# Hybrid encoder on one core: rotary tables into a slab, gates' exchange between the rotary products, P4's last sum one unit sooner, memory values later

## The chip, the cores and the metric

The kernel runs on one core of one Trainium2 chip. Its engines are named here as the profile names them: PE (TensorE, matrix products; PEld is its weight load), DVE (VectorE), ACT (ScalarE), POOL (GpSimd) and SP (SyncE, which only issues transfers here). The metric is the device time in microseconds (us) of one execution, lower is better. A time of a kernel is the median of several executions.

## The reference

The kernel computes two layers of an encoder over 512 positions of width 2048. Cut to what matters here:

```python
for l in range(DEPTH):                                        # DEPTH = 2
    h = rmsnorm(x, pre_norm_g[l])
    z = h @ w_in[l]
    q_lat, kv_lat, k_pe, gb, gc, xin, q_mem, gate = split_cols(z)
    q = (rmsnorm(q_lat, q_norm_g[l]) @ w_uq[l])               # 8 heads, 128 + 64 rotary columns each
    q = concatenate([q[..., :128], apply_rope(q[..., 128:], cos, sin)])
    kv = rmsnorm(kv_lat, kv_norm_g[l]) @ w_ukv[l]             # keys and values, 8 heads
    a_out = mla_attention(q, k, v)                            # softmax over 512 positions
    c_out = short_gated_conv(gb, gc, xin, conv_w[l])
    m_out = memory_attention(q_mem, mem_n, w_mk[l], w_mv[l])  # 4 heads into 256 memory rows
    y = concatenate([a_out, c_out, m_out]) * silu(gate)
    x = x + rmsnorm(y @ w_o[l], post_norm_g[l])
```

Everything is in float32.

## The kernel before, in words

**Products in three parts.** A float32 operand is split into a rounded high part and the rest, a low part; a product is three matmuls, high x high, high x low and low x high (lines 272, 273 and 274, helper `mm3`). The high part is a cast on ACT, the low part a subtraction on DVE. For weights these are lines 189 (tile `wh`) and 190 (tile `wl`); other operands are split by `split_to` (lines 277 and 278).

**Groups, products and units.** The input projection is worked in groups of columns, two tiles of tokens at a time, with seven products of block sums, P1 to P7, in place of eight (as Strassen's method does). Each product has four units, c = 0 to 3, one for each chunk of 512 rows of the weights. A unit gives 12 matmuls of 512 columns (two token tiles, two halves of the chunk, three parts). Its weights come by `load` on SP's queue into a raw buffer (`wr`, 8 of them, line 146), or are added to a buffer by an accumulating transfer on POOL's queue (`more`). Where neither fits, two buffers are added on DVE: `sums` (line 178) ahead of the unit's split, `then` (line 199) behind it. There are three `wh` and three `wl` tiles, 8 banks for sums of products, and 19 large tiles called slabs.

**The last group, g4.** It makes the gates `ga0` and `ga1`. It has `spared` set (as has, in layer 1 alone, the second group): in P4 its last unit has its second block (B21) loaded on SP and added by line 178, where other units use an accumulating transfer. The steps of this group are numbered; a table `beside` puts other work behind steps 12 to 27. Steps 20 to 23 are P7, 24 to 27 are P4. That other work is: the latents' rows turned through an exchange (`latents_rows_out`, 32x3x128 transfers into the slabs `D1` and `D2`), their split in four parts into `H1`, `H2` (high) and `D1`, `D2` (low) by `latents_split(0..3)`, the memory keys' fetch (`mem_fetch("Km")`), the exchange of the conv-side gates (`gate_rows(3, "gm")`, 16 transfers on SP into a slab `y`), the shared rotary key's transposes (`k_rope_turn`, `krps`), and the fetch of the rotary tables (`tables_fetch`, tile `tab`, into a raw buffer).

**The mixer behind it.** `mixer` puts the first of two rotary products (`p0`, banks `qr`, weights `w_qr`), the last latents' split, the memory values' fetch (`Vm`), the second rotary product, an activation that loads ACT's table for the exponential, the rotation on DVE (`rotate0`: `first` line 1145, `second` lines 1149 and 1150, `both` lines 1154 and 1155, `away` a split and a way through DRAM to the tile `QR`), then the first query products (`qps`, tile `Q`) and the heads: four memory heads, four token tiles each, then eight latent heads. One head tile is: scores on PE (`sc`), their negated maximum on DVE (line 1260, `nm`), the exponential on ACT (line 1263), its sum's reciprocal on DVE (line 1265, `rec`), the normalisation on ACT (line 1266), transposes on PE (line 1276, `ptp`), a split of these (`PT`), and the product with the values (`o`). `y` is the gate rows times `o` (line 1291).

**What sets the order.** PE, SP and POOL run their instructions in the order in which the program puts them. On DVE and ACT a scheduler orders the instructions ahead of time; each of the two engines then runs its list in order and waits at an instruction whose input is not there. `tc.keep_in_program_order` pins an instruction into the program's order. A DMA issue whose buffer is still in use holds up everything behind it on its queue.

Of the kernel before, what the change touches and what calls it, by code (L numbers as in the profile page):

```python
# [5 lines left out]
F32 = mybir.dt.float32  # L6
# [3 lines left out]
ALU = mybir.AluOpType  # L10
# [75 lines left out]
class Program:  # L86
# [23 lines left out]
    def add(self, fn, units=(), room=0.0, ahead=None):  # L110

        self.steps.append((list(units), fn, room, self.ahead if ahead is None else ahead))
# [115 lines left out]
def encoder(tc, x, xt, mem, memt, positions, columns, conv_w, w_in, q_norm_g, w_uq, w_qr, kv_norm_g, w_ukv,  # L228
# [47 lines left out]
    def split_to(hi, lo, src):  # L276
        nc.scalar.copy(hi, src)
        nc.vector.tensor_tensor(lo, src, hi.bitcast(F32), op=ALU.subtract)
# [213 lines left out]
    def group(left, key, w, block, slot, passes, final, hold=None, by_two=False, direct=None, spared=False, once=False):  # L492
# [25 lines left out]
        def unit(q, c):  # L518
            k = lambda n: (key, n, c)

            def of(name, loads=(), more=None, sums=(), then=(), **kw):
                at = {"B11": (0, 0), "B12": (0, 1), "B21": (1, 0), "B22": (1, 1)}
                return Unit(k(name), {k(to): [block(*at[n], c)] for to, n in loads}, more and block(*at[more], c),
                            [(k(a), k(b)) for a, b in sums], [(k(a), k(b)) for a, b in then], **kw)
            if q == "P1":
                to = "P1" if apart and not keep else "T"
                return of(to, [(to, "B11")])
            if q == "P2":
                return of("P2", [("P2", "B21")])
            if q == "P4" and c == 3 and spared:  # L530
                return of("T", [("B21", "B21")], sums=[("T", "B21")])
            if q == "P4":
                return of("T", more="B21", alloc=hold, behind=(key, "B22", 3) if passes is SECOND and c > 1 else None)
            if late:
                return {"P5": lambda: of("T", [("B12", "B12")], sums=[("T", "B12")], place=place),
                        "P6": lambda: of("T", [("B22", "B22")], sums=[("T", "B22")]),
                        "P3": lambda: of("B22", then=[("B12", "B22")]),
                        "P7": lambda: of("B12")}[q]()
            if q == "P5" and (passes is STEADY or passes is FIRST):
                return of("T", [("T", "B11")] * (passes is FIRST) + [("B12", "B12")], sums=[("T", "B12")])  # L540
            if once and q in ("P6", "P3"):
                return of("T", [("B22", "B22")], sums=[("T", "B22")]) if q == "P6" else of("B22")
            return {"P5": lambda: of("T", [("T", "B11")] if apart and not keep else [], more="B12"), "P6": lambda: of("T", more="B22"),
                    "P3": lambda: of("B22", [("B22", "B22")]), "P7": lambda: of("B22", more="B12")}[q]()
# [363 lines left out]
    def mem_fetch(n, k):  # L908
        def f():
            t = slab(n, F32R)  # L910
            nc.gpsimd.dma_start(t, G[n + "d"])
            G[n] = t.rearrange("p (s i c) -> p s i c", s=2, i=k)
        return f
# [160 lines left out]
            exchange(C["D"][k].rearrange("p (c n) -> p c n", n=S)[:, :3], C["lat"][k][:, :, :12], queue, (p,))  # L1074
        return f

    def latents_split(n, C):
        def f():
            if n == 0:
                C["H"] = slab("H1", F32R), slab("H2", F32R)  # L1080
            (d1, d2), (h1, h2) = C["D"], C["H"]
            hi, lo = ((h1[:, :768], d1[:, :768]), (h1[:, 768:1536], d1[:, 768:1536]), (h1[:, 1536:], d2[:, :512]),
                      (h2[:, :1024], d2[:, 512:1536]))[n]
            split_to(hi, lo.bitcast(F32R), lo)
            if n == 2:
                k = lambda t, c: t[:, c * S:(c + 1) * S]
                l1, l2 = (d.bitcast(F32R) for d in (d1, d2))
                G["cq"] = [k(h1, c) for c in range(4)], [k(l1, c) for c in range(3)] + [k(l2, 0)]
                G["ckv"] = [k(h2, c) for c in range(2)], [k(l2, c) for c in (1, 2)]
        return f  # L1090
# [28 lines left out]
    def halves(name, dt=F32):  # L1119
        return raw_p.tile([P, 1024], dt, tag="raw", name=nm(name)).rearrange("p (s c) -> p s c", s=2)  # L1120

    def tables_fetch():
        G["tab"] = halves("tab")
        nc.gpsimd.dma_start(G["tab"].rearrange("p s c -> p (s c)"), G["tabd"])

    def q_rope_steps(l, g):
# [213 lines left out]
    def mixer(l, C, pair2, tail):  # L1340

        (p0, rotate0, fetch0), (p1, rotate1, fetch1) = (q_rope_steps(l, g) for g in range(2))
        put(p0[:1])
        add(latents_split(3, C))
        add(mem_fetch("Vm", 2))
        put(p0[1:])
        add(lambda: nc.scalar.activation(small(1, "ex"), C["ga0"][:, NT - 1][:, 0, :1], AF.Exp, scale=0.0))
        put(rotate0[:2])
        sts = [{} for _ in range(4)]
        qkv = qkv_steps(l, 0, sts[0])  # L1350
        qkv[0] += (0.0, 1)
        qkv[2] += (0.0, 0)
        put(qkv[:1])
        its = [it for i in range(4) for it in mem_head(i)]
        m = len(its)
        between = {k: [s] for k, s in zip((2, 5, 8, 10, 12), qkv[1:])}
        between.setdefault(6, []).append((gate_rows(0, "ga0", C), []))
        for k, s in zip((1, 3), rotate0[2:]):
            between.setdefault(k, []).append(s)
        between.setdefault(7, []).append((fetch0, []))  # L1360
        between.setdefault(12, []).append((gate_rows(1, "ga1", C), []))
        between[m - 2] = [(lambda: pr.prep_next(), [])]
        for pair in range(4):
            for i in range(2):
                its += mla_head(2 * pair + i, sts[pair])
            nxt = tail if pair == 3 else spread(8, qkv_steps(l, pair + 1, sts[pair + 1]))
            if pair == 0:
                nxt = dict(zip((-1, 1, 3, 4, 6, 7), nxt_steps(nxt)))
            if pair == 2:
                nxt.update(pair2)  # L1370
            for k, v in nxt.items():
                between.setdefault(m + 8 * pair + k, []).extend(v)
        between.setdefault(m + 2, []).append((conv_rows(C), []))
        late = [(4, (tables_fetch, [])), (5, p1[0]), (6, p1[1])] + list(zip((6, 7, 8, 9), rotate1)) + [(11, (fetch1, []))]
        if l + 1 < depth:
            late += zip((12, 14, 16, 17, 18, 19, 20, 21), mem_turned_steps(l + 1))
        for k, s in late:
            between.setdefault(m + k, []).append(s)
        pipeline(its, between, m)
# [169 lines left out]
    for l in range(depth):  # L1549
# [117 lines left out]
        if l == 0:  # L1667
# [22 lines left out]
            12: out_(0, 0, q=sy), 13: out_(0, 1, q=sy), 14: out_(0, 2, q=sy), 15: out_(0, 3, q=sy),  # L1690
            16: out_(1, 0, q=sy), 17: out_(1, 1, q=sy), 18: [qm_split(0, C)] + out_(1, 2, q=gp),
            19: [qm_split(1, C)] + out_(1, 3, q=gp), 20: [lambda C=C: k_rope(C)],
            21: [latents_split(0, C)], 22: [latents_split(1, C)], 24: [latents_split(2, C), mem_fetch("Km", 4)],
            25: [gate_rows(3, "gm", C)], 26: [k_rope_turn(C), tables_fetch],
        }
        for n in range(12, 28):
            put(g4[n:n + 1])
# [88 lines left out]
```

## Time and profile before

| | us |
|---|---|
| median of 3 executions | 1459.48 |
| lowest and highest of them | 1458.66, 1460.37 |
| profiled execution, its own time | 1457.07 |
| span of the profiled execution | 1455.2 |
| granted TensorE clock, mean | 0.999 |
| mean transfer rate | 205 GB/s |

The profiled execution is a single one. Its span runs from the first to the last recorded instruction; its own time has 1.9 us around that. A timeline row gives start, duration, engine, line, operation, output tile and input tiles, and the form of these; in brackets stands the idle time of the engine ahead of it and what ended that. Layer 0's P4 lies at 411 to 425 us and its memory heads begin at 433; in layer 1 the same places lie at 1134 and 1156.

### The profile page before, as it was taken

The numbers are of one execution on the slowest core, as the hardware profiler recorded it, in microseconds if no ns is written. First come the engines' busy times: TensorE is split into PE (matmuls) and PEld (weight loads), VectorE is DVE, ScalarE is ACT, GpSimd is POOL, SyncE is SP. The second block draws the span as 40 slices with busy tenths as digits, with TensorE's granted clock in tenths as the row PEclk, the third lists the DMA queues.
The fourth block names the chain that finished last, engine by engine and source line by source line (L and its number), as shares of the span: only waits on it lengthen the run. The fifth ranks groups of instructions, "written<-read, shape, count | busy, mean of one in ns | idle before, by whom it ended". The sixth has DMA issues, their size and how long they took to land.

```text
span 1455.2 us, 19537 instructions
## 1 busy us (share of the span) xinstructions
PE 1434.8 (99%) x6960; PEld 1222.0 (84%) x6960; DVE 1129.2 (78%) x1546; ACT 872.5 (60%) x1358; POOL 283.6 (19%) x321
## 2 busy tenths in 40 slices
PE   9999999999999999999999999999999999999997
PEld 8888888898877888888898888888988788888886
DVE  5899687967877778868879666977588776788687
ACT  7856345446558688654777434544465586776543
POOL 0032403032301100311210333030333001003111
PEclk9999999999999999999999999999999999999999
DMA  9999979697896482795987999696969876129973
GB/s 366 415 265 221 223 191 206 157 203 216 187 263 166 133 260 87 135 242 147 339 285 230 233 229 222 198 192 173 208 197 191 252 174 155 35 84 159 280 154 130
DMA packets 166210, 298.44 MB, mean 205 GB/s; under 512 B 13696, under 2 KB 57760, under 8 KB 162272
## 3 DMA queue, kind: packets, MB, share of 16 engines
q0 software_dynamic: 54736, 122.51, 41.5%
q1 hardware_dynamic: 111376, 174.67, 38.1%
q8 instruction: 55, 0.90, 0.2%
q14 instruction: 43, 0.35, 0.1%
HBM read 261.85 MB, written 21.63 MB: 195 GB/s over the span
## 4 chain that ended last, share of the span: by engine, by line
PE 91%; DMA 3%; DVE 3%; ACT 2%; issue 1%; SPq 1%; POOL 0%; POOLq 0%; DVEq 0%; ACTq 0%
PE P L273 22%; PE P L274 22%; PE P L272 22%; PE ptp L1276 2%; PE o L273 1%; PE o L272 1%; PE o L274 1%; PE sc L272 1%; PE sc L273 1%; PE sc L274 1%; PE qps L272 1%; PE qps L274 1%; PE sc L1258 1%; PE sc L1257 1%; PE qps L273 1%; DVE wl L190 1%
## 5 line engine op out<-in xcount | busy, mean ns | idle before, releaser
L189 ACT CAST wh<-wr 128x1024 fp32r<-128x1024 f32 (+2 forms) x436 | 444.9, 1023 | 419.5 <-PE P L274 309.7
L190 DVE TENSOR_TENSOR wl<-wr,wh 128x1024 fp32r<-128x1024 f32 (+2 forms) x436 | 514.6, 1184 | 215.8 <-ACT wh L189 213.1
L273 PE MATMUL P<-wl,S 128*128 128x512 f32 (+1 forms) x896 | 344.1, 384 | 0.2
L272 PE MATMUL P<-wh,S 128*128 128x512 f32 (+1 forms) x896 | 344.0, 384 | 0.0
L274 PE MATMUL P<-wh,S 128*128 128x512 f32 (+1 forms) x896 | 343.3, 383 | 0.0
L273 PE MATMUL P<-wl,A 128*128 128x512 f32 (+1 forms) x656 | 252.1, 384 | 2.3 <-DVE wl L190 2.3
L272 PE MATMUL P<-wh,A 128*128 128x512 f32 (+1 forms) x656 | 253.0, 386 | 0.6 <-ACT ga L589 0.6
L274 PE MATMUL P<-wh,A 128*128 128x512 f32 (+1 forms) x656 | 251.6, 384 | 0.0
L146 POOL DMA_DIRECT2D wr<-in_w_in_dram x121 | 145.2, 1200 | 411.4 <-DVE wl L190 193.8
L273 PEld LDWEIGHTS P<-wl,S 128*128 128x128 f32 x896 | 168.2, 188 | 31.1 <-DVE wl L190 1.3
L274 PEld LDWEIGHTS P<-wh,S 128*128 128x128 f32 x896 | 168.2, 188 | 30.2
L272 PEld LDWEIGHTS P<-wh,S 128*128 128x128 f32 x896 | 168.2, 188 | 30.1
L273 PEld LDWEIGHTS P<-wl,A 128*128 128x128 f32 x656 | 123.2, 188 | 25.0 <-DVE wl L190 3.5
L272 PEld LDWEIGHTS P<-wh,A 128*128 128x128 f32 x656 | 123.1, 188 | 23.2 <-ACT ga L589 1.4
L274 PEld LDWEIGHTS P<-wh,A 128*128 128x128 f32 x656 | 123.2, 188 | 22.1
L146 POOL DMA_DIRECT2D wr<-in_w_o_dram x40 | 48.5, 1259 | 298.0 <-DVE wl L190 294.3
L1263 ACT ACTIVATE P<-sc,nm 128x512 f32<-128x512 f32 (+1 forms) x96 | 59.4, 620 | 26.9 <-DVE nm L1260 26.6
L1260 DVE TENSOR_REDUCE nm<-sc 128x1 f32<-128x512 f32 (+1 forms) x96 | 56.9, 593 | 12.7 <-PE sc L1258 9.2
L1266 ACT ACTIVATE P<-P,rec 128x512 f32<-128x512 f32 (+1 forms) x96 | 61.6, 657 | 6.8 <-DVE rec L1265 6.8
L178 DVE TENSOR_TENSOR wr<-wr,wr 128x1024 f32<-128x1024 f32 (+1 forms) x47 | 55.6, 1183 | 7.2 <-DMA wr<-in_w_in_dram 6.8
L1276 PE MATMUL ptp<-identr,P 128*128 128x128 f32 x320 | 46.3, 273 | 6.6 <-ACT P L1266 6.6
L1276 PEld LDWEIGHTS ptp<-identr,P 128*128 128x128 f32 x320 | 37.9, 140 | 13.6 <-ACT P L1266 7.8
(322 smaller groups left out, 2096.9 us busy)
## 6 DMA issues: line engine op xcount, KB each, us to landing
wr<-in_w_in_dram SPq DMA_DIRECT2D x131, 512.0 KB, 4.9
wr<-in_w_in_dram POOLq DMA_DIRECT2D x97, 512.0 KB, 7.4
wr<-in_w_o_dram SPq DMA_DIRECT2D x48, 512.0 KB, 6.3
wr<-in_w_o_dram POOLq DMA_DIRECT2D x40, 512.0 KB, 7.2
wr<-in_w_in_dram SPq DMA_DIRECT2D x32, 416.0 KB, 3.7
wr<-in_w_in_dram POOLq DMA_DIRECT2D x24, 416.0 KB, 5.9
wr<-in_w_mk_dram SPq DMA_DIRECT2D x15, 512.0 KB, 8.1
wr<-in_w_mv_dram SPq DMA_DIRECT2D x15, 512.0 KB, 10.1
```

The lines of the kernel that those rows point to most:

```text
L146: engine.dma_start(dst, src, **kw)
L178: nc.vector.tensor_tensor(tiles[a], tiles[a], tiles[b], op=ALU.add)
L189: pin(nc.scalar.copy(hi[:, h], src[:, h]))
L190: pin(nc.vector.tensor_tensor(lo[:, h], src[:, h], hi[:, h].bitcast(F32), op=ALU.subtract))
L272: nc.tensor.matmul(ps, ah, bh, start=first, stop=False, **kw)
L273: nc.tensor.matmul(ps, ah, bl, start=False, stop=False, **kw)
L274: nc.tensor.matmul(ps, al, bh, start=False, stop=last, **kw)
L1257: nc.tensor.matmul(ps, q, G["KA"], start=False, stop=False)
L1260: nc.vector.tensor_reduce(nmax, ps, axis=AX.X, op=ALU.max, negate=True)
L1263: nc.scalar.activation(pt, ps, AF.Exp, bias=nmax, accum_out=tot)
L1266: nc.scalar.activation(pt, pt, AF.Copy, scale=rec)
L1276: nc.tensor.transpose(ps[:, k * P:(k + 1) * P], pt[:, k * P:(k + 1) * P], G["ident"])
```

## The change

P4's unit c = 2 of the spared groups loads the last unit's second block as well, and adds it behind its own split; unit c = 3 only splits. The rotary tables' first fetch goes into a slab and is put behind step 21 (P7) rather than 26 (P4). The memory keys' fetch goes from step 24 to 23. The exchange of `gm` goes from step 25 into the mixer, between the two rotary products. The last latents' split is pinned into program order, on both engines. A new small POOL operation reads a column of the third tile of `ga0` ahead of the memory values' fetch, so that the fetch is issued only after that tile is written.

```diff
@@ -528,7 +528,10 @@
             if q == "P2":
                 return of("P2", [("P2", "B21")])
             if q == "P4" and c == 3 and spared:
-                return of("T", [("B21", "B21")], sums=[("T", "B21")])
+                return of("T")
+            if q == "P4" and c == 2 and spared:
+                t, b = ((key, n, 3) for n in ("T", "B21"))
+                return Unit(k("T"), {b: [block(1, 0, 3)]}, block(1, 0, 2), then=[(t, b)])
             if q == "P4":
                 return of("T", more="B21", alloc=hold, behind=(key, "B22", 3) if passes is SECOND and c > 1 else None)
             if late:
@@ -1074,14 +1077,15 @@
             exchange(C["D"][k].rearrange("p (c n) -> p c n", n=S)[:, :3], C["lat"][k][:, :, :12], queue, (p,))
         return f
 
-    def latents_split(n, C):
+    def latents_split(n, C, pin=lambda ins: ins):
         def f():
             if n == 0:
                 C["H"] = slab("H1", F32R), slab("H2", F32R)
             (d1, d2), (h1, h2) = C["D"], C["H"]
             hi, lo = ((h1[:, :768], d1[:, :768]), (h1[:, 768:1536], d1[:, 768:1536]), (h1[:, 1536:], d2[:, :512]),
                       (h2[:, :1024], d2[:, 512:1536]))[n]
-            split_to(hi, lo.bitcast(F32R), lo)
+            pin(nc.scalar.copy(hi, lo))
+            pin(nc.vector.tensor_tensor(lo.bitcast(F32R), lo, hi.bitcast(F32), op=ALU.subtract))
             if n == 2:
                 k = lambda t, c: t[:, c * S:(c + 1) * S]
                 l1, l2 = (d.bitcast(F32R) for d in (d1, d2))
@@ -1119,8 +1123,8 @@
     def halves(name, dt=F32):
         return raw_p.tile([P, 1024], dt, tag="raw", name=nm(name)).rearrange("p (s c) -> p s c", s=2)
 
-    def tables_fetch():
-        G["tab"] = halves("tab")
+    def tables_fetch(first=False):
+        G["tab"] = slab("tab")[:, :1024].rearrange("p (s c) -> p s c", s=2) if first else halves("tab")
         nc.gpsimd.dma_start(G["tab"].rearrange("p s c -> p (s c)"), G["tabd"])
 
     def q_rope_steps(l, g):
@@ -1341,8 +1345,10 @@
 
         (p0, rotate0, fetch0), (p1, rotate1, fetch1) = (q_rope_steps(l, g) for g in range(2))
         put(p0[:1])
-        add(latents_split(3, C))
+        add(latents_split(3, C, tc.keep_in_program_order))
+        add(lambda: nc.gpsimd.tensor_scalar(small(1, "ms"), C["ga0"][:, 2][:, 0, :1], 1.0, None, op0=ALU.mult))
         add(mem_fetch("Vm", 2))
+        add(gate_rows(3, "gm", C))
         put(p0[1:])
         add(lambda: nc.scalar.activation(small(1, "ex"), C["ga0"][:, NT - 1][:, 0, :1], AF.Exp, scale=0.0))
         put(rotate0[:2])
@@ -1690,8 +1696,8 @@
             12: out_(0, 0, q=sy), 13: out_(0, 1, q=sy), 14: out_(0, 2, q=sy), 15: out_(0, 3, q=sy),
             16: out_(1, 0, q=sy), 17: out_(1, 1, q=sy), 18: [qm_split(0, C)] + out_(1, 2, q=gp),
             19: [qm_split(1, C)] + out_(1, 3, q=gp), 20: [lambda C=C: k_rope(C)],
-            21: [latents_split(0, C)], 22: [latents_split(1, C)], 24: [latents_split(2, C), mem_fetch("Km", 4)],
-            25: [gate_rows(3, "gm", C)], 26: [k_rope_turn(C), tables_fetch],
+            21: [latents_split(0, C), lambda: tables_fetch(True)], 22: [latents_split(1, C)],
+            23: [mem_fetch("Km", 4)], 24: [latents_split(2, C)], 26: [k_rope_turn(C)],
         }
         for n in range(12, 28):
             put(g4[n:n + 1])
```

In layer 1's second group the add keeps its place in DVE's order and only has another line (199 for 178). On PE the order is the same before and after. Three places where it differs follow, all in layer 0; layer 1 has the same. An order's row gives line, operation, output and input tiles, their shape, and how many alike follow each other.

DVE, at the end of P4. `wl160` to `wl163` are the low parts of P4's units c = 0 to 3, `wr91` is the last unit's buffer and `wr104` the block that is added to it, `D1` and `D2` are parts of the latents' split. Before:

```order
L190 TENSOR_TENSOR wl160_3582<-wr88_2871,wh160_3581 128x1024
L278 TENSOR_TENSOR D1_136_3355<-D1_136_3355,H1_144_3575 128x768
L278 TENSOR_TENSOR D2_137_3356<-D2_137_3356,H1_144_3575 128x512
L190 TENSOR_TENSOR wl161_3603<-wr89_2889,wh161_3602 128x1024
L590 SCALAR_TENSOR_TENSOR ga1_117_3039<-ga1_117_3039,ga0_116_3038 128x16x32 x2
L178 TENSOR_TENSOR wr91_2942<-wr91_2942,wr104_3496 128x1024
L939 STREAM_TRANSPOSE ga1_117_3039<-ga1_117_3039 128x16x32 x2
L190 TENSOR_TENSOR wl162_3629<-wr90_2907,wh162_3628 128x1024
L190 TENSOR_TENSOR wl163_3652<-wr91_2942,wh163_3651 128x1024
```

And in the changed kernel:

```order
L190 TENSOR_TENSOR wl160_3584<-wr88_2871,wh160_3583 128x1024
L1088 TENSOR_TENSOR D1_136_3355<-D1_136_3355,H1_144_3575 128x768
L199 TENSOR_TENSOR wr91_2942<-wr91_2942,wr104_3471 128x1024
L190 TENSOR_TENSOR wl161_3605<-wr89_2889,wh161_3604 128x1024
L593 SCALAR_TENSOR_TENSOR ga1_117_3039<-ga1_117_3039,ga0_116_3038 128x16x32 x2
L190 TENSOR_TENSOR wl162_3633<-wr90_2907,wh162_3632 128x1024
L942 STREAM_TRANSPOSE ga1_117_3039<-ga1_117_3039 128x16x32 x2
L1088 TENSOR_TENSOR D2_137_3356<-D2_137_3356,H1_144_3575 128x512
L190 TENSOR_TENSOR wl163_3654<-wr91_2942,wh163_3653 128x1024
```

The add into `wr91` has moved from between `wl161` and `wl162` to ahead of `wl161` (line 199 for 178); the `D2` part of 512 columns has moved from ahead of `wl161` to ahead of `wl163`, and the two transposes of `ga1` behind `wl162`.

DVE, where the memory heads begin. `rm` and `qr` are the rotation's tiles, `Q` the low part of the first queries, `nm` and `rec` the heads' maxima and reciprocals, `wl166` and `wl167` low parts of weights for the heads' projections. Before:

```order
L190 TENSOR_TENSOR wl166_3743<-wr107_3579,wh166_3742 128x1024
L190 TENSOR_TENSOR wl167_4170<-wr108_3599,wh167_4169 128x1024
L1260 TENSOR_REDUCE nm_159_3804<-sc_158_3800 128x1
L1145 TENSOR_TENSOR rm_155_3778<-qr_151_3746,tab_150_3715 128x1024
L278 TENSOR_TENSOR Q_156_3784<-qps_157_3785,Q_156_3784 128x512
L1149 TENSOR_TENSOR qr_151_3746<-qr_153_3763,tab_150_3715 128x512
L1150 TENSOR_TENSOR qr_153_3763<-qr_153_3763,tab_150_3715 128x512
L1265 RECIPROCAL rec_162_3809<-tot_161_3807 128x1
L1260 TENSOR_REDUCE nm_164_3816<-sc_163_3812 128x1
L1154 TENSOR_TENSOR rm_155_3778<-rm_155_3778,qr_153_3763 128x512
L1155 TENSOR_TENSOR rm_155_3778<-rm_155_3778,qr_151_3746 128x512
L1265 RECIPROCAL rec_167_3821<-tot_166_3819 128x1
```

And in the changed kernel:

```order
L190 TENSOR_TENSOR wl166_3726<-wr107_3581,wh166_3725 128x1024
L1088 TENSOR_TENSOR D2_137_3356<-D2_137_3356,H2_145_3576 128x1024
L1149 TENSOR_TENSOR rm_156_3780<-qr_150_3729,tab_146_3579 128x1024
L1153 TENSOR_TENSOR qr_150_3729<-qr_154_3765,tab_146_3579 128x512
L1154 TENSOR_TENSOR qr_154_3765<-qr_154_3765,tab_146_3579 128x512
L1159 TENSOR_TENSOR rm_156_3780<-rm_156_3780,qr_150_3729 128x512
L1158 TENSOR_TENSOR rm_156_3780<-rm_156_3780,qr_154_3765 128x512
L190 TENSOR_TENSOR wl167_4172<-wr108_3601,wh167_4171 128x1024
L278 TENSOR_TENSOR Q_157_3786<-qps_158_3787,Q_157_3786 128x512
L1264 TENSOR_REDUCE nm_160_3806<-sc_159_3802 128x1
L1264 TENSOR_REDUCE nm_165_3818<-sc_164_3814 128x1
L1264 TENSOR_REDUCE nm_170_3832<-sc_169_3828 128x1
```

The rotation's five operations have moved from between the first maximum and the second reciprocal to ahead of `wl167` and `Q`; the last latents' split (`D2`, 1024 columns) now stands ahead of the rotation.

SP and POOL, the queues. `wr108` to `wr115` are weights of the heads' projections and of the rotary products, and blocks of the memory rows (`in_memt_dram`). SP before:

```order
L146 DMA wr108_3599<-in_w_uq_dram 128x4x128 x2
L146 DMA wr109_3626<-in_w_ukv_dram 128x2x512
L146 DMA wr110_3648<-in_w_qr_dram 128x1024
L947 DMA y_147_3667<-gm_86_1836 32x4x128 x16
L146 DMA wr111_3684<-in_w_uq_dram 128x4x128 x2
L146 DMA wr112_3717<-in_w_ukv_dram 128x2x512
L146 DMA wr113_3740<-in_memt_dram 128x512
L146 DMA wr114_3782<-in_memt_dram 128x512
L146 DMA wr115_3906<-in_w_uq_dram 128x4x128 x2
```

And in the changed kernel:

```order
L146 DMA wr108_3601<-in_w_uq_dram 128x4x128 x2
L146 DMA wr109_3630<-in_w_ukv_dram 128x2x512
L146 DMA wr110_3651<-in_w_qr_dram 128x1024
L146 DMA wr111_3669<-in_w_uq_dram 128x4x128 x2
L146 DMA wr112_3700<-in_w_ukv_dram 128x2x512
L146 DMA wr113_3723<-in_memt_dram 128x512
L950 DMA y_153_3748<-gm_86_1836 32x4x128 x16
L146 DMA wr114_3784<-in_memt_dram 128x512
L146 DMA wr115_3908<-in_w_uq_dram 128x4x128 x2
```

The 16 transfers of the gates' exchange have moved behind three loads. On POOL, before:

```order
L947 DMA D2_137_3356<-lat_98_2431 32x3x128 x8
L911 DMA Km_146_3646<-Kmd0_795 128x2048
L1124 DMA tab_150_3715<-tabd_2925 128x1024
L911 DMA Vm_152_3761<-Vmd0_723 128x2048
L1163 DMA qrd0_0_3868<-qrh_179_3865 128x2x512
```

And in the changed kernel:

```order
L950 DMA D2_137_3356<-lat_98_2431 32x3x128 x8
L1128 DMA tab_146_3579<-tabd_2925 128x1024
L914 DMA Km_147_3628<-Kmd0_795 128x2048
L1349 TENSOR_SCALAR ms_151_3744<-ga0_116_3038 128x1
L914 DMA Vm_152_3746<-Vmd0_723 128x2048
```

The tables' fetch has moved ahead of the memory keys', and the new operation (`ms`) stands ahead of the values'.

## The prediction

> **What bounds the kernel now.** I read the page first, for the busy shares:
>
> ```profile
> span 1455.2 us, 19537 instructions
> PE 1434.8 (99%) x6960; PEld 1222.0 (84%) x6960; DVE 1129.2 (78%) x1546; ACT 872.5 (60%) x1358; POOL 283.6 (19%) x321
> ```
>
> PE (matmul) idles for 1455.2 − 1434.8 = 20.4 us in all. The change adds and removes no matmul, so it can only touch these. The view of waits, for PE alone, says who ended that idle time (line waited with, producer, total us, times, longest):
>
> ```profile
> PE ptp L1276 <- ACT P L1266: 6.6, 6, 1.5
> PE P L273 <- DVE wl L190: 2.3, 2, 1.1
> PE P L272 <- ACT ga L589: 0.6, 2, 0.4
> ```
>
> The table by windows says where (length, busy us of PE, PEld, DVE, ACT, POOL with counts, granted clock, DMA share, GB/s):
>
> ```profile
> 410.00:424.00 14.00, 12.48 (x58) 9.71 (x57) 13.10 (x14) 9.52 (x14) 1.08 (x2) 1.00 0.88 265
> 436.00:447.00 11.00, 7.70 (x47) 6.29 (x46) 9.55 (x27) 9.52 (x29) 3.68 (x6) 1.00 0.53 183
> 470.00:1100.00 630.00, 629.88 (x3066) 539.32 (x3066) 483.03 (x615) 375.25 (x565) 131.11 (x145) 1.00 0.80 205
> 1130.00:1146.00 16.00, 14.65 (x68) 11.54 (x68) 12.79 (x14) 10.59 (x14) 1.08 (x2) 1.00 0.92 276
> 1158.00:1170.00 12.00, 8.70 (x52) 7.15 (x51) 10.07 (x29) 10.21 (x32) 3.66 (x6) 1.00 0.72 234
> ```
>
> Elsewhere PE is full (0.12 idle in 630 us). In each layer it idles twice: 1.5 us at the end of the gates' last product P4 (410 to 424), and 3.3 us at the start of the memory heads (436 to 447). All the edits lie around these. PE's timeline shows the single stalls (start, us, instruction, in brackets the idle time before it and its releaser):
>
> ```profile
> 411.69 0.50 PE L272 MATMUL P<-wh,A 128*128 128x512 f32 x1 [0.39 <-ACT ga L589]
> ...
> 417.27 0.39 PE L272 MATMUL P<-wh,A 128*128 128x512 f32 x1
> 418.79 0.50 PE L273 MATMUL P<-wl,A 128*128 128x512 f32 x1 [1.13 <-DVE wl L190]
> ...
> 424.94 0.39 PE L272 MATMUL qr<-H,wh 128*128 128x512 f32 x1
> ...
> 438.16 0.44 PE L1276 MATMUL ptp<-identr,P 128*128 128x128 f32 x2 [0.73 <-ACT P L1266]
> 440.42 0.44 PE L1276 MATMUL ptp<-identr,P 128*128 128x128 f32 x2 [1.46 <-ACT P L1266]
> 444.86 0.44 PE L1276 MATMUL ptp<-identr,P 128*128 128x128 f32 x2 [1.11 <-ACT P L1266]
> 1141.15 0.50 PE L273 MATMUL P<-wl,A 128*128 128x512 f32 x1 [1.14 <-DVE wl L190]
> ```
>
> The last row is layer 1's P4 stall, of the same size; the waits view counts each kind twice or six times. So I work out layer 0 and double it.
>
> **P4's last sum, one unit sooner.** VectorE (DVE), which writes wl, is full there:
>
> ```profile
> 410.25 1.22 DVE L190 TENSOR_TENSOR wl<-wr,wh 128x1024 fp32r<-128x1024 f32 x1 [2.78 <-ACT wh L189]
> 411.39 1.55 DVE L278 TENSOR_TENSOR D<-D,H 128x768 fp32r<-128x768 f32 x2
> 412.86 1.22 DVE L190 TENSOR_TENSOR wl<-wr,wh 128x1024 fp32r<-128x1024 f32 x1
> 414.00 1.28 DVE L590 SCALAR_TENSOR_TENSOR ga<-ga,ga 128x512 f32<-128x512 f32 x2
> 415.20 1.22 DVE L178 TENSOR_TENSOR wr<-wr,wr 128x1024 f32<-128x1024 f32 x1
> 416.33 1.29 DVE L939 STREAM_TRANSPOSE ga<-ga 128x512 f32<-128x512 f32 x2
> 417.56 2.31 DVE L190 TENSOR_TENSOR wl<-wr,wh 128x1024 fp32r<-128x1024 f32 x2
> ```
>
> The third wl, which PE waits for at 418.79, starts at 417.56, behind the sum and two transposes. Nothing is removed from DVE: the add (1.14 by its distance to the next row) moves ahead of c=1's split, and the D part of 512 columns moves behind the third wl. Laid out with these durations the new order is: wl of c=0 to 411.4, one D part (0.8) to 412.2, the add to 413.4, wl of c=1 to 414.5, ga x2 to 415.7, wl of c=2 to 416.9, transposes to 418.1, D to 418.7, wl of c=3 to 419.9. PE wants the wl of c=2 at 417.27 + 0.23 = 417.50: **met with 0.6 to spare**. It wants that of c=1 13 starts after 411.69 (24 starts from there to 417.27 are 5.58, or 0.2325 each), at 414.7: met, but with only 0.2 to spare. The stall goes; PE gains the distance 418.79 − 417.50 = 1.29 and the slow first matmul (0.50 for 0.39), together 1.4. The 0.39 wait at 411.69 is on ScalarE (ACT), behind a cast that the change leaves; I count nothing for it. Does the add's data come in time, or does DVE now stall for a load? SP issues it early:
>
> ```profile
> 399.50 1.83 SPq L146 DMA_DIRECT2D wr<-in_w_in_dram  x1
> wr<-in_w_in_dram SPq DMA_DIRECT2D x1, 512.0 KB, 7.5
> ```
>
> The second row, from the DMA view of 398 to 412, is its time from issue to landing. 399.5 + 7.5 = 407.0, or 408.8 from the issue's end; the add starts at 412.2. Bounds of this part: 0 (c=1's wl takes the stall over) and 1.6 (stall, restart and a shorter wait at 421). I take **1.4 per layer**, the row's own value.
>
> One rule of the Trainium skill prices the regained stretch higher. The page "TensorE: Matmul & The Clock Gate", section "Wait — 56ns, not 53.3ns?", gives 215.7 ns from start to start for warm matmuls of 512 columns; the rows above give 232.5 here. By the page the 24 matmuls from 417.27 to 424.94 could also lose 24 × 17 ns = 0.4, so 1.8 per layer and 0.8 us more in total. The rows are slower than the page, so the sum goes by them.
>
> **Tables sooner; the rotary products off the softmax's path.** At the memory heads' start DVE has this order:
>
> ```profile
> 431.48 1.23 DVE L190 TENSOR_TENSOR wl<-wr,wh 128x1024 fp32r<-128x1024 f32 x1 [3.55 <-ACT wh L189]
> 433.65 0.42 DVE L1260 TENSOR_REDUCE nm<-sc 128x1 f32<-128x256 f32 x1 [0.94 <-PE sc L274]
> 433.99 1.21 DVE L1145 TENSOR_TENSOR rm<-qr,tab 128x1024 f32<-128x1024 f32 x1
> 435.12 0.68 DVE L278 TENSOR_TENSOR Q<-qps,Q 128x512 fp32r<-128x512 f32 x1
> 435.72 0.69 DVE L1149 TENSOR_TENSOR qr<-qr,tab 128x512 f32<-128x512 f32 x1
> ...
> 436.92 0.15 DVE L1265 RECIPROCAL rec<-tot 128x1 f32<-128x1 f32 x1
> ```
>
> ACT's timeline shows what that costs:
>
> ```profile
> 434.17 0.48 ACT L1263 ACTIVATE P<-sc,nm 128x256 f32<-128x256 f32 x1 [0.29 <-DVE nm L1260]
> ...
> 437.60 0.51 ACT L1266 ACTIVATE P<-P,rec 128x256 f32<-128x256 f32 x1
> ```
>
> The first exponential is done by 434.8, but its reciprocal runs at 436.92, behind two rotary products, a split and a third, and PE's first transpose waits for the normalisation that follows. Meanwhile DVE sat idle for 3.55 us before 431.48. POOL fetched the table late:
>
> ```profile
> 420.18 0.54 POOL L1124 DMA_DIRECT2D tab<-tabd  x1 [14.13 <-DVE wl L190]
> ```
>
> It had waited 14 us there for a raw buffer that a wl freed. Into a slab it goes five steps sooner, and the new order has all five rotary operations ahead of the wl at 431.48, in the idle time. With everything 1.4 sooner, PE ends the second rotary product at 429.1; the four operations behind it take 4 × 0.6 to 431.5; wl to 432.7, Q to 433.3, three maxima of 0.33 to 434.3. ACT's exponential follows the first maximum at 433.6 and ends by 434.2, a second by 434.8; then the two normalisations, done by 435.3 and 435.8. PE wants the first at 438.16 − 0.73 − 1.4 = 436.0 and the second some 0.6 later. **Both waits go: 0.73 + 1.46 = 2.2.** The third (1.11) I leave standing: PE comes 3.6 sooner, and ACT, busy 9.52 of 11 us there, has the same work before that transpose. Bounds: 0 (chain as long as before) and 3.3 (all three gone). I take **2.2 per layer**. What hides it is the 3.55 us gap; if the gap closed, half of the rotary work (2.5 us) would be back in the chain.
>
> **The gates' exchange.** 16 issues on SP move behind three loads:
>
> ```profile
> 416.88 13.66 SPq L947 DMA_DIRECT2D y<-gm  x16
> ...
> DMA to landing us min/median/max: 2.0/6.5/8.5
> ...
> 449.18 0.69 DVE L1291 TENSOR_TENSOR y<-o,y 128x512 f32<-128x512 f32 x1
> ```
>
> (SP's timeline, tile y from 410 to 450, DVE's timeline.) The last load ahead of it waits for the rotary weight's wl, about 421.3 in the new order, so the exchange runs from 421.5 to 435.2 and lands by 443.7 with the slowest landing. DVE's product y wants it at 449.18 − 3.6 = 445.6: covered by 1.9. Cost 0; behind it on SP stand a memory load and the next uq loads, which are not used before y. The loads that pass it gain some 14 us of lead, which no PE wait asks for.
>
> **Memory values later, ScalarE's and VectorE's split pinned.** The new POOL operation on one column has its nearest row in the chain of waits:
>
> ```profile
> 352.74 0.25 POOL r L1045
> ```
>
> It holds the values' fetch until a gate tile of P4 is turned, near 423.5. With the 7.5 that a weight took to land, doubled for its double size, the values are there by 439; o, which ends just before y at 445.6, is the first to use them: cost 0, and at the most 0.25 on an engine that is 19% busy. Pinning latents 3's split changes order, not work. Km's fetch, one step sooner in the program, waits behind the same transfers: 0.
>
> **Sum.** −(1.4 + 2.2) × 2 = **−7.2 us**. The profiled execution took 1457.07 (span 1455.2 and 1.9 around it), so it would take 1449.9. The runs shown have a median of 1459.48, 2.4 above it; against that: 1459.48 − 7.2 = **1452.3 us**.
>
> **Rivals.**
> - All the named waits go, the third transpose's and ACT's 0.4 too: 6.6 + 2.3 + 0.6 = 9.5, so 1450.0. Against: ACT's load at the third transpose is untouched. Chance 0.08.
> - Only P4 gains; the transposes still wait, since ACT, not the reciprocal, ends the chain: −2.8, 1456.7. For: ACT is 87% busy in 436 to 447; against: in 434.8 to 436.9 the chain waited for DVE, not for ACT. Chance 0.12.
> - Only the heads gain; P4's stall moves to c=1's wl, whose margin is 0.2: −4.4, 1455.1. Chance 0.06.
> - Nothing net: each wait is replaced by one as long a few units on (the change doesn't do what it says), 1459.5. Chance 0.08.
> - **Slower**: the gates' exchange lands late. Its 16 issues now start 4.6 us later and share the queue with the loads; y on DVE holds up the K and PT splits behind it, which PE needs. Every us beyond 445.6 costs one per layer; it eats the gain from 449.2 on and passes 0.2% from 450.7, so the landing must slip 7 us beyond my estimate. At 451.7 the time is 1459.5 + 2 × 2.5 = 1464.5. For: the exchange takes 0.85 us an issue (13.66 / 16), so a queue that is held up between issues slips by the sum; against: the DMA share is 0.53 after 436. Chance 0.08.
>
> **How the numbers follow.** 0.2% (2.9 us, so 1456.6) is about what a measurement of this kernel can tell from no change. Forecast 0.58, all waits 0.08, heads alone 0.06 are faster: 0.72. P4 alone and nothing net are the same: 0.20. Slower 0.08. The range reaches from all waits gone less the runs' own 0.9 (1449.0) to P4 alone plus 0.8 (1457.5); outside lie nothing net and slower, 0.16.
>
> **What would show it.** In the new trace P4's wait of PE on wl near 418 and 1141 is gone, and the first rotary matmul starts near 423.5; DVE's rotary operations end before the first maximum; ptp waits fall from 6.6 to about 2.2 or 2.5 in two instances; y's first product starts unhindered near 445.6. I am wrong if c=1's wl stalls PE, if DVE shows idle time ended by the y exchange or by wr, or if the normalisation, with its reciprocal early, still ends the waits.

## The result and the profile after

| | before | changed |
|---|---|---|
| median, us | 1459.80 (6 runs, 1458.66 to 1462.71) | 1452.18 (6 runs, 1450.35 to 1454.28) |
| ratio, 95% interval | 1 | 0.9947 (0.9933 to 0.9961) |
| profiled execution: own time, span | 1457.07, 1455.2 | 1452.78, 1450.6 |

The change takes 7.6 us off the median; 1452.3 us and −7.2 were forecast. In a second set of runs, beside three of the experiments, the ratio was 0.9941 (0.9929 to 0.9954). The number was right, but one of the two reasons behind it was not, as the experiments show. The ratios leave out one execution, of the kernel with the third split pinned, that took 1588.41 us at a granted clock of 0.85.

The view of waits for PE, changed kernel (total us, times, longest us); `ptp` are the transposes, `ga` the copy that P4's first matmul waits for:

```profile
PE P L272 <- ACT ga L592: 2.4, 2, 1.9
...
PE ptp L1280 <- ACT P L1270: 1.0, 2, 0.5
PE P L273 <- DVE wl L190: 0.9, 3, 0.6
PE sc L272 <- ACT P L1267: 0.6, 2, 0.3
```

Against before, the transposes' waits fell from 6.6 to 1.0 with a new 0.6 on `sc` (−5.0), and P4's two waits on wl (2.3) are gone. On the other side the wait at P4's start grew from 0.6 to 2.4, and three small waits on wl, 0.9 together, appear in places where the two programs do the same. Sum: −5.0 − 2.3 + 1.8 + 0.9 = −4.6, which is also the difference of the two spans.

So the traces account for 4.6 us, and the medians differ by 7.6. Most of the rest lies in the kernel before: its profiled execution took 1457.07 us, 2.7 less than the median of its runs, and what the other executions lose is in no trace. Their granted clock gives a hint: it is below 0.998 in 23 of the 57 executions of the kernel before that ran beside the experiments, and in none of 11 of the changed kernel; the ten executions of before at 0.996 average 1461.8 us, the fourteen at 0.999 average 1459.4.

The windows that were read before, in the changed kernel (columns as there):

```profile
410.00:424.00 14.00, 13.48 (x65) 10.82 (x64) 11.99 (x13) 10.06 (x14) 0.00 (x0) 1.00 0.97 330
436.00:447.00 11.00, 10.21 (x64) 8.60 (x63) 8.05 (x24) 10.96 (x35) 3.71 (x6) 1.00 0.57 186
1130.00:1146.00 16.00, 14.12 (x68) 11.31 (x67) 12.82 (x15) 11.03 (x16) 0.47 (x2) 1.00 0.89 288
1158.00:1170.00 12.00, 11.21 (x76) 9.76 (x74) 10.12 (x30) 10.84 (x35) 3.69 (x6) 1.00 0.87 230
```

PE is 10.21 of 11 us busy at the heads (7.70 before). ACT is now full there, 10.96 of 11. The third window has PE idle for 1.88 us, more than before: this is the wait at P4's start in layer 1. PE's own timeline has it, and where the stretches begin:

```profile
413.03 0.50 PE L272 MATMUL P<-wh,A 128*128 128x512 f32 x1 [0.52 <-ACT ga L592]
...
424.78 0.39 PE L272 MATMUL qr<-H,wh 128*128 128x512 f32 x1
...
442.05 0.44 PE L1280 MATMUL ptp<-identr,P 128*128 128x128 f32 x2 [0.51 <-ACT P L1270]
...
1133.25 0.50 PE L272 MATMUL P<-wh,A 128*128 128x512 f32 x1 [1.88 <-ACT ga L592]
```

The first row is P4's start. From there to the first rotary matmul (second row) it takes 424.78 − 413.03 = 11.75 us, against 424.94 − 411.69 = 13.25 before: −1.5.

DVE's timeline there shows the order that was laid out by hand, and its starts: the add, the wl of c = 1 and the wl of c = 2.

```profile
413.59 1.22 DVE L199 TENSOR_TENSOR wr<-wr,wr 128x1024 f32<-128x1024 f32 x1
414.72 1.22 DVE L190 TENSOR_TENSOR wl<-wr,wh 128x1024 fp32r<-128x1024 f32 x1
415.86 1.29 DVE L593 SCALAR_TENSOR_TENSOR ga<-ga,ga 128x512 f32<-128x512 f32 x2
417.06 1.22 DVE L190 TENSOR_TENSOR wl<-wr,wh 128x1024 fp32r<-128x1024 f32 x1
```

The wl of c = 2 starts 4.0 us after P4's start, against 5.9 before.

At the heads' start the rotation (lines 1149 to 1159) is over before the first maximum, and the reciprocal follows the maxima (DVE's timeline, changed kernel):

```profile
428.82 1.22 DVE L1149 TENSOR_TENSOR rm<-qr,tab 128x1024 f32<-128x1024 f32 x1
430.42 0.70 DVE L1153 TENSOR_TENSOR qr<-qr,tab 128x512 f32<-128x512 f32 x1 [0.37 <-PE qr L274]
...
434.55 1.08 DVE L1264 TENSOR_REDUCE nm<-sc 128x1 f32<-128x256 f32 x3
435.66 0.16 DVE L1269 RECIPROCAL rec<-tot 128x1 f32<-128x1 f32 x1
```

The exchange (SP's timeline) and the first product that needs it (DVE's timeline), changed kernel:

```profile
422.80 13.70 SPq L950 DMA_DIRECT2D y<-gm  x16
...
446.28 0.69 DVE L1295 TENSOR_TENSOR y<-o,y 128x512 f32<-128x512 f32 x1
```

y starts without a wait.

### The profile page after: what moved, and what is told of

Same layout as the page of the kernel before. It is cut to its first block, busy times and chain, and to the rows that moved or that the text cites. A ratio compares the mean times of both kernels' runs of the same rounds, so it can differ in the third digit from the quotient of the medians.

```text
span 1450.6 us, 19532 instructions
## 1 busy us (share of the span) xinstructions
PE 1435.3 (99%) x6960; PEld 1222.5 (84%) x6960; DVE 1129.7 (78%) x1546; ACT 871.9 (60%) x1358; POOL 285.0 (20%) x323
## 4 chain that ended last, share of the span: by engine, by line
PE 89%; DMA 3%; issue 3%; DVE 1%; ACT 1%; POOL 1%; SPq 1%; POOLq 0%; ACTq 0%; DVEq 0%
PE P L272 21%; PE P L273 21%; PE P L274 21%; PE ptp L1280 2%; DMA wr<-in_w_in_dram 2%; PE o L273 1%; PE o L274 1%; PE o L272 1%; PE sc L272 1%; PE sc L273 1%; PE sc L274 1%; PE qps L274 1%; PE sc L1261 1%; PE qps L272 1%; PE sc L1262 1%
## 5 line engine op out<-in xcount | busy, mean ns | idle before, releaser
L178 DVE TENSOR_TENSOR wr<-wr,wr 128x1024 f32<-128x1024 f32 (+1 forms) x44 | 52.0, 1183 | 5.7 <-DMA wr<-in_w_in_dram 5.0
```

The costliest lines, as they stand in the source:

```text
L178: nc.vector.tensor_tensor(tiles[a], tiles[a], tiles[b], op=ALU.add)
```

## The experiments

A hunk is one piece of the change that can be built alone. Theory A is the prediction's: the early tables free the rotation, the exchange's move costs and brings nothing. Theory B came from the orders of kernels with one edit each: DVE's list has the rotation early if the exchange is moved, whatever is done to the tables. Ratios are against the kernel before, in runs on the same chip.

| kernel | median, us | ratio (95%) | waits: P4 on wl, ptp and sc, P4's start |
|---|---|---|---|
| before | 1459.80 | 1 | 2.3, 6.6, 0.6 |
| changed | 1452.18 | 0.9947 (0.9933 to 0.9961) | 0, 1.6, 2.4 |
| P4's sum alone | 1454.99 | 0.9962 (0.9949 to 0.9974) | 0, 5.2, 2.0 |
| exchange alone | 1456.70 | 0.9978 (0.9969 to 0.9987) | 2.2, 1.6, 3.6 |
| tables alone | 1460.74 | 1.0001 (0.9993 to 1.0010) | 2.3, 5.2, 1.3 |
| all but the exchange | 1455.64 | 0.9965 (0.9953 to 0.9977) | 0, 5.2, 1.6 |
| all but the tables | 1451.40 | 0.9944 (0.9931 to 0.9956) | 0, 1.6, 0.8 |
| all but P4's sum | 1454.88 | 0.9965 (0.9953 to 0.9977) | 2.3, 1.6, 2.3 |
| changed kernel again | 1451.60 | 0.9941 (0.9929 to 0.9954) | 0, 1.6, 0.9 |
| rotation put back | 1455.26 | 0.9971 (0.9960 to 0.9982) | 0, 4.6, 0.8 |
| third split pinned | 1449.58 | 0.9929 (0.9915 to 0.9942) | 0, 1.6, 0 |
| three edits | 1450.07 | 0.9935 (0.9922 to 0.9948) | 0, 1.6, 0 |
| exchange one load later | 1452.85 | 0.9947 (0.9934 to 0.9960) | 0, 1.0, 1.1 |
| exchange two loads later | 1463.53 | 1.0024 (1.0010 to 1.0038) | 0, 7.4, 0.5 |

The waits are those of each kernel's one profiled execution, in us, both layers together; of the waits on wl, those at P4's stall (1.1 us each) alone, and in the last two rows also what waits on Q, PT and in `vps` at the heads.

**P4's sum alone** (`only_sum`): the kernel before with

```diff
-                return of("T", [("B21", "B21")], sums=[("T", "B21")])
+                return of("T")
+            if q == "P4" and c == 2 and spared:
+                t, b = ((key, n, 3) for n in ("T", "B21"))
+                return Unit(k("T"), {b: [block(1, 0, 3)]}, block(1, 0, 2), then=[(t, b)])
```

> The kernel before with P4's last sum one unit sooner, nothing else. Both theories: P4's wait of PE on wl (1.1 us in each layer) goes, the heads keep their ptp waits of 3.3 us a layer: about -2.8 us, 0.998 of before. If c=1's wl took the stall over, PE would show a wait on wl half a unit after P4's start and the time would not change.

P4's stall went in both layers. The gain, 5.1 us between medians, is larger than expected. A part of that is shown: DVE's list changed further on too, so that one rotary product ran ahead of the first maximum, and ptp waits fell from 6.6 to 5.2. With the stall that is 3.7 us; where the rest comes from no trace shows.

**Exchange alone** (`only_gm`):

```diff
-            25: [gate_rows(3, "gm", C)], 26: [k_rope_turn(C), tables_fetch],
+            26: [k_rope_turn(C), tables_fetch],
...
         add(mem_fetch("Vm", 2))
+        add(gate_rows(3, "gm", C))
```

> The kernel before with only the gates' exchange put between the two rotary products; the tables still come late and into a raw buffer. Theory A (the prediction's: the early tables free the rotation from the softmax's path): DVE's rotation still waits for the table, ptp waits stay at 6.6 us, 0 us. Theory B (DVE's list is what counts, and it is the exchange's place that changes the list; the table, issued at 420 and landing before 430, is early enough in both): the rotation runs ahead of the first maximum, ptp waits fall to about 1.5 us, -4.4 us or a little more, 0.997 of before; P4's wl stall stays.

Theory B. The tables are issued late, at 423.69 us (POOL's timeline), and the rotation still runs early and without a wait for them (DVE's timeline):

```profile
423.69 0.54 POOL L1124 DMA_DIRECT2D tab<-tabd  x1 [15.57 <-DVE wl L190]
...
431.47 1.23 DVE L1145 TENSOR_TENSOR rm<-qr,tab 128x1024 f32<-128x1024 f32 x1
434.03 0.70 DVE L1149 TENSOR_TENSOR qr<-qr,tab 128x512 f32<-128x512 f32 x1 [1.33 <-PE qr L274]
```

The ptp and sc waits fall by 5.0; of this the medians show 3.4 (1.9 to 4.5 by the interval), and this execution's waits at P4's start are 3.0 longer than in the profile of before.

**Tables alone** (`only_tab`): the kernel before with (lines cut to the entries that differ)

```diff
-            21: [latents_split(0, C)], 22:
+            21: [latents_split(0, C), lambda: tables_fetch(True)], 22:
...
-26: [k_rope_turn(C), tables_fetch],
+26: [k_rope_turn(C)],
```

and `tables_fetch(first)` as in the change.

> The kernel before with only the tables fetched at P7 into a slab. Theory A: the heads' gain comes with this edit alone, -4.4 us, ptp waits near 2. Theory B: the first reciprocal still stands behind rotary products in DVE's list, ptp waits stay near 6.6, 0 us (within 1).

No gain: theory A falls. DVE's idle time of 3.55 us stays ahead of a wl, and the rotation, though its tables have long landed, follows that wl in the list:

```profile
434.41 1.23 DVE L190 TENSOR_TENSOR wl<-wr,wh 128x1024 fp32r<-128x1024 f32 x1 [3.55 <-ACT wh L189]
435.55 1.22 DVE L1145 TENSOR_TENSOR rm<-qr,tab 128x1024 f32<-128x1024 f32 x1
```

The heads' three waits have become one of 2.59 us in each layer (below).

**All but the exchange** (`no_gm`) and **all but the tables** (`no_tab`), the changed kernel with the hunk of the experiment ahead undone (`-` and `+` exchanged), the exchange's in the first and the tables' in the second:

> The changed kernel with the gates' exchange back behind step 25. Theory A: the exchange costs and brings nothing, so the whole gain stays: -7.2 us. Theory B: only P4's part stays, -2.8 us, ptp waits back near 6.6 us.

> The changed kernel with the tables fetched as before, at step 26 into a raw buffer. Theory A: the rotation waits for the table on DVE, ptp waits near 6.6, -2.8 us. Theory B: DVE's list has the rotation early all the same, the table lands in time; -7.5 us, as the changed kernel. A third outcome: the raw buffer that the table holds again delays a weight, seen as a PE wait on wl behind 430.

Both go theory B's way. Without the exchange's move ptp waits are those of P4's sum alone (5.2) and the time is too; with the tables late, time and waits are the changed kernel's.

**All but P4's sum** (`no_sum`), the changed kernel with the diff on P4 undone:

> The changed kernel with P4's last sum as before. P4's waits on wl (1.1 us in each layer) come back, ptp waits stay near 0.5 a layer: 2.3 to 2.8 us slower than the changed kernel, -4.7 to -5.2 against before. If P4's stall had gone for another reason (the pinned split, the earlier loads), -7.5 against before.

P4's stall is back (1.14 and 1.15 us) and 2.7 to 3.3 us of time are lost against the changed kernel, by the medians of its two sets of runs. The sum's part and the exchange's add up within their intervals: −5.1 and −3.4 alone, −7.6 together.

**Changed kernel again** (`changed_again`):

> The changed kernel once more, beside the next three on one chip. About -7.5 us, 0.995 of before. In this profile the wait of PE at P4's start (on the copy of ga) should again be larger than the 0.4 and 0.2 us of before in at least one layer, if it hangs on when the latents' exchange lands, which differs from execution to execution.

One wait of 0.86 at P4's start in layer 0, none to speak of in layer 1, where the first profile had 1.88. So much of that size belongs to the execution and not to the change.

**Rotation put back** (`turn_between`): what does the work, DVE's list or the weights that now pass the exchange on SP? The queues stay as in the changed kernel; the rotation's steps are called from within the first two memory scores and pinned, as are the maxima, the reciprocals and the second Q there.

```diff
-        put(rotate0[:2])
+        add(lambda: G.update({("turn", 12, 0): [f for f, _ in rotate0[:2]], ("turn", 12, 1): [rotate0[2][0]]}))
...
-                nc.vector.tensor_reduce(nmax, ps, axis=AX.X, op=ALU.max, negate=True)
+                pin(nc.vector.tensor_reduce(nmax, ps, axis=AX.X, op=ALU.max, negate=True))
+                for f in G.pop(("turn", j, t), ()):
+                    f()
```

> The changed kernel with every queue as it is there, but the rotation's five operations pinned on DVE between the first memory maximum and the second reciprocal, as in the kernel before. Theory B1 (the gain at the heads is DVE's list alone): ptp waits return to about 3 us in each layer, the time is that of the P4 edit alone or worse: -3 us against before. Theory B2 (the gain comes from the weights that now pass the exchange on SP's queue): ptp waits stay near 0.8 us a layer, -7.5 us.

The heads' first two waits come back with 0.73 and 1.57 us, for 0.73 and 1.46 before (PE's timeline):

```profile
436.98 0.44 PE L1287 MATMUL ptp<-identr,P 128*128 128x128 f32 x2 [0.73 <-ACT P L1277]
439.34 0.47 PE L1287 MATMUL ptp<-identr,P 128*128 128x128 f32 x2 [1.57 <-ACT P L1277]
```

With SP's queue as in the changed kernel 3.7 us are lost. So it is the list (theory B1). The third wait of before (1.11) does not come back; DVE's list behind the second reciprocal was not put back.

**Third split pinned** (`split2_pin24`): the wait at P4's start, taken up.

```diff
-            23: [mem_fetch("Km", 4)], 24: [latents_split(2, C)], 26: [k_rope_turn(C)],
+            23: [mem_fetch("Km", 4)], 24: [latents_split(2, C, tc.keep_in_program_order)], 26: [k_rope_turn(C)],
```

> The changed kernel with the third part of the latents' split pinned to its place in the program (step 24), so that on ScalarE its cast stands behind the two copies of ga at P4's start. If PE's wait on that copy (0.5 and 1.9 us in the changed kernel's profile) comes from the cast that waits for the latents' exchange, the wait goes in both layers: -1 to -2.4 us against the changed kernel, about -9.3 against before. If the copy is late for another reason (PE's own end of P7, or wl), nothing changes.

The wait is gone in both layers, and 2.0 us come off the changed kernel beside it, to the lowest median of all kernels here. ACT's timeline shows why. In the changed kernel the cast to H waits 3.41 us for the latents' exchange and holds up two casts and the copy of ga behind it:

```profile
409.97 0.62 ACT L1087 CAST H<-D 128x512 fp32r<-128x512 f32 x1 [3.41 <-DMA D<-lat]
410.50 2.00 ACT L189 CAST wh<-wr 128x1024 fp32r<-128x1024 f32 x2
412.40 1.06 ACT L592 COPY ga<-P 128x512 f32<-128x512 f32 x2
```

With the pin the copy runs when P7 ends, and the cast later, without a wait:

```profile
410.88 0.59 ACT L592 COPY ga<-P 128x512 f32<-128x512 f32 x1 [0.26 <-PE P L274]
...
414.73 0.61 ACT L1087 CAST H<-D 128x512 fp32r<-128x512 f32 x1
```

**Three edits** (`three_edits`): the kernel before with P4's sum, the exchange's move and the two last splits pinned; all fetches as before (lines cut to the entries that differ).

```diff
-24: [latents_split(2, C), mem_fetch("Km", 4)],
+24: [latents_split(2, C, tc.keep_in_program_order), mem_fetch("Km", 4)],
...
-        add(latents_split(3, C))
+        add(latents_split(3, C, tc.keep_in_program_order))
```

> The kernel before with three things only: P4's last sum one unit sooner, the gates' exchange between the rotary products, and both last parts of the latents' split pinned to the program. Tables, memory keys and memory values are fetched as before. If those fetches are worth nothing, the time is that of the changed kernel with the third part pinned (0.993 of before, -10 us). If the tables' slab or the delayed values are needed for it, a wait on wr, tab or Vm shows and up to 2 us are lost.

0.9935 against 0.9929, with intervals that overlap: the three fetches (tables, keys, values) are worth nothing that can be measured here. The pin of the last split was not built alone; the exchange alone has its gain without it.

**Exchange one load later** (`gm_later`) and **two loads later** (`gm_far`): the changed kernel without the line that is taken out here; the first has it behind `put(qkv[:1])`, the second in `between`:

```diff
-        add(gate_rows(3, "gm", C))
...
         put(qkv[:1])
+        add(gate_rows(3, "gm", C))
...
+        between.setdefault(5, []).append((gate_rows(3, "gm", C), []))
         between.setdefault(6, []).append((gate_rows(0, "ga0", C), []))
```

> The changed kernel with the gates' exchange put one place further on, behind the first query product, so that on SP it follows the next load too (issued at 436.6 in the changed kernel). The slower rival's mechanism: the exchange is then issued from 437 to 451 and lands about 456; DVE's y, wanted at 446, holds up the splits behind it, PE stalls by 8 to 11 us in each layer, about 1452 + 16 to 22 = 1468 to 1474, and DVE shows idle time ended by the y exchange. Against it: if the splits behind y leave PE room, the stall is shorter or none, 1452.

The expected slip failed to come: the load that now stands ahead of the exchange, and in the changed kernel had queued behind it, was issued by 430.2, the exchange from 430.5 to 442.1, and y waited 0.2 us. Counted from P4's start, the exchange ended 3.6 us later than in the changed kernel, at no cost. y itself came 1.1 us later there, by another list, so the room in the changed kernel is some 2 to 3 us, for the 1.9 of the prediction.

> The changed kernel with the gates' exchange put behind the load that follows it on SP in the run before (issued at 442.3 there), just ahead of ga0's exchange. By that run's pace (16 issues in 11.6 us) it is issued from 443.5 to 455 and lands about 458; DVE's first y, which ran at 449.4 with 0.2 us of idle time there, would start some 9 us late. If the slower rival's mechanism holds at its price (one to one, in both layers), the time is about 1452 + 18 = 1470 (1464 to 1476), and DVE's idle time ahead of y ends with the exchange's transfers. If PE has room behind y, the loss is well below 9 us a layer.

Here it is slower than before. The load was issued sooner than expected, so the exchange ran from 438.5 to 451.7, and DVE's y waits for it (DVE's timeline):

```profile
453.17 0.69 DVE L1295 TENSOR_TENSOR y<-o,y 128x512 f32<-128x512 f32 x1 [1.03 <-DMA y<-gm]
```

Counted from the first rotary matmul, y is 8 us late. PE's waits at the heads are 5.8 us longer than in the changed kernel's profile (7.4 for 1.6), both layers together, and not 8 in each. Nor do they all come from the late exchange. In each layer the first two end before y starts (PE's timeline, layer 0):

```profile
447.70 0.38 PE L272 MATMUL sc<-Km,QmH 128*128 128x256 f32 x1 [0.90 <-ACT P L1267]
449.43 0.39 PE L272 MATMUL vps<-wh,H 128*128 128x256 f32 x1 [1.11 <-ACT P L1267]
```

They wait for the heads' exponentials (line 1267), these for the maxima, and these for the scores; by the timelines no transfer stands in that chain. DVE's list is another one here: y stands behind two maxima, two reciprocals, three splits of PT and one of V that follow it with the exchange one load later. These waits are 4.0 of the 7.4 us in both layers; those behind y, on PT, are 3.1. What a late landing alone would cost stays open. The profiled executions differ by 8.8 us of span, the medians by 11.4; the part that is not waiting is taken up in the last section.

## Why the prediction was right or wrong

- **P4's sum: right.** The stall went as laid out in both layers: from P4's start to its end it takes 1.5 us less in layer 0 and 1.4 in layer 1, for the 1.4 forecast; c = 1's wl, with its margin of 0.2, was never waited for.
- **Tables: wrong step, right size.** The prediction wrote "Into a slab it goes five steps sooner, and the new order has all five rotary operations ahead of the wl", and took the first for the cause of the second. Tables alone bring nothing; the exchange's move alone brings the new list. The chain from list to PE was right: it gave 2.2 a layer, and the profile shows 3.3 of waits becoming 0.8, that is 2.5. It could have been seen beforehand from DVE's order in a kernel with one hunk. How the scheduler arrives at its list from the exchange's place was not tried.
- **Third transpose: too high.** Its wait was left at 1.1 in each layer; 0.5 and a 0.3 on `sc` remained. ACT is full there, as said.
- **Exchange: "Cost 0" was right for the queue, and wrong as its worth:** its move alone brought 3.4 us. Its two ends, 421.5 and 435.2 forecast, were 422.8 and 436.5; y was forecast at 445.6 and ran at 446.3, without a wait.
- **P4's start: "I count nothing" left out what moves most from run to run.** 0.4 and 0.2 us in the profile of before, 0.5 and 1.9 in the changed kernel's. It took back 1.8 us of the profiled execution's gain; the changed kernel's second profile has 0.9. The cause is the cast that waits for the latents' exchange on ACT, ahead of the copy: pinned behind it, the wait is gone and 2.0 us with it. The prediction saw the cast and left it, as the change does.
- **Slower rival:** with the exchange 16 us later the kernel is slower than before (by 0.2%), as it said, and y waits for the exchange. Its price, one to one, was not found, and more than half of the waits stand ahead of y, in a list that is another one. Where the loss begins was not measured.
- **Memory values, keys, tables:** together nothing that can be measured; 0 was forecast for the first two.
- **The match of the sum: in part luck.** The waits that went are 7.3 us in the profile, for the 7.2 of the sum, but of these 2.2 a layer were credited to the wrong edit, and 2.7 came back in that execution. The medians agree with the forecast because the other executions of the kernel before lose more than its profiled one, which no row had shown.

## What to carry to other kernels

A transfer's place in a program can matter through the list that a scheduler then makes for an engine whose work at that place does not use it; build each hunk alone and read the order before crediting an edit with what the whole diff does. A chain of small waits behind one engine is priced from that engine's list, operation by operation. An operation that waits for a late transfer holds up everything listed behind it: put it behind the work that PE is about to need (here 2.0 us for one pin).

## What the runs showed of the hardware

After PE stalls of 0.9 to 2.6 us the granted clock can fall, and that can cost nearly as much again. With the tables alone, PE's timeline shows a wait of 2.59 us, and from 0.6 us after it matmuls of 512 columns start every 0.43 us in place of 0.23, for 3.1 us:

```profile
442.95 0.44 PE L1276 MATMUL ptp<-identr,P 128*128 128x128 f32 x2 [2.59 <-ACT P L1266]
...
445.02 0.63 PE L273 MATMUL kps<-D,wh 128*128 128x512 f32 x1
445.45 0.63 PE L274 MATMUL kps<-H,wl 128*128 128x512 f32 x1
```

The windows of this kernel have a granted clock of 0.80 there, and those of the exchange two loads later reach 0.50 (the granted clock is the third number from the end):

```profile
440.00:446.00 6.00, 3.41 (x18) 2.92 (x17) 4.59 (x13) 5.95 (x19) 1.46 (x2) 0.80 0.30 121
450.00:452.00 2.00, 2.00 (x11) 2.00 (x11) 1.59 (x4) 1.69 (x6) 0.00 (x0) 0.50 0.41 106
```

The second row follows the stalls of 0.90 and 1.11 us shown above. In that last kernel PE is busy 1440.7 us, against 1435.3 for the same matmuls in the changed kernel: 5.4 us. With the 5.8 of waits at the heads, less the 2.5 by which the waits at P4's start and on wl are shorter in this execution, that makes up 8.7 of the 8.8 us by which its span is longer.

It is not in every stall, and the length alone does not decide: before, 0.73, 1.46 and 1.11 us within 7 us left the clock at 1.00, and so did the longest wait of the exchange alone, at P4's start (all windows of 1 us from 408 to 430 have 1.00):

```profile
415.20 0.50 PE L272 MATMUL P<-wh,A 128*128 128x512 f32 x1 [2.31 <-ACT ga L589]
```

In the kernel with the rotation put back two stalls as before's first two (0.73 and 1.57 us) brought it to 0.80 in layer 0 and left it at 1.00 in layer 1 (windows):

```profile
436.00:442.00 6.00, 3.70 (x18) 2.91 (x17) 5.90 (x17) 5.75 (x16) 1.49 (x2) 0.80 0.36 135
...
1158.00:1164.00 6.00, 3.71 (x25) 3.14 (x25) 5.82 (x18) 5.89 (x17) 1.48 (x2) 1.00 0.63 209
```

The Trainium skill, on its page "TensorE: Matmul & The Clock Gate", Part 1, lets the clock fall after an idle window of some 3.4 us. The rows here have it fall after a gap of 2.59 us, and after 0.90 and 1.11 us, with PE busy before and after, so here the measurement decides. The lower clock of the Trainium skill on that page, half of the full one, agrees with the 0.50.

A forecast that counts waits alone can so be too low: the tables alone took 1.4 us off the heads' waits and nothing off the time, and PE was busy 1439.4 us there, against 1434.8 before.
